# Hybrid encoder block on one core: where the casts of weights that are split ahead stand in ScalarE's order of issue

## The chip, the cores and the metric

The kernel runs on one core of a Trainium2 chip. A core has a matrix engine (TensorE, PE in the profile; PEld is its weight load), a vector engine (VectorE, DVE), a scalar engine (ScalarE, ACT), a general engine (GpSimd, POOL), a queue that only issues transfers (SyncE, SP), and sixteen DMA engines shared by all queues. The metric is device microseconds of the whole program, the median of several runs.

## The reference, cut to what matters

One layer of a streaming encoder works on 1024 tokens of width 1024, in float32. The part that this change touches is the input projection and what reads it:

```python
xn = rmsnorm(x, norm1_g[layer])
u = xn @ w_in[layer].astype(f32)
q_sb, k_sb, v_sb, f_raw, i_hg, q_hg, g_hg, gate_sb, gate_hg = jnp.split(u, list(c), axis=-1)
o_sb = stick_breaking_attention(split_heads(q_sb, SB_HEADS), ...)   # 8 heads of 64
o_hg = hgrn2_chunkwise(silu(q_hg), k_hg, i_hg, log_f)               # 4 heads of 128
merged = g_a * (o_sb @ w_o_sb) + g_b * (o_hg @ w_o_hg)
h = x + merged @ w_out
h = h + square(relu(rmsnorm(h) @ w_ff1)) @ w_ff2                    # width 4096
return rmsnorm(h, final_g)
```

Each w_in column block is used once, against all 1024 tokens.

## The kernel before, in words

**Split matmuls.** Every large product is made of three matmuls in a reduced format (`three`, L490). An operand becomes a high part h, cast by ScalarE (`hi_copy`, L141), and a low part l = x - h, subtracted by VectorE (`lo_sub`, L144). `hi_lo` (L150) does both. A tile of weights is 128 x 1024, so each split is one ScalarE cast and one VectorE subtraction.

**Units and buffers.** A `Unit` (L385) holds one block of weights. `load` (L401) brings the raw tile from memory into one of two buffers with the tag "raw"; `split` (L414) makes h and l in one of two buffers each, tags "whi" and "wlo". Wide units (`wide_unit`, L530: wv0, wv1, wi0, wi2) have two raw pieces and put their halves into the pool of 40 slots instead, so they hold no whi buffer. A `RawUnit` (L1110, wga0 to wga7, the gate weights) loads two raw tiles, splits one of them, subtracts twice in place and splits half of the result (`split_t`, tile t).

**Jobs.** `Stream` (L435) is the list of projection jobs. Its order is: wqk0 with wv0, wqk1 to wqk4, wv1, wqk5 to wqk7, then wf0, wq0, wi0, wg0, wf1, wq1, wg1, wga0, wf2, wq2, wi2, wg2, wga1, wga2, wf3, wq3, wg3, wga3 to wga7, wo00 to wo03. When a job starts (`_start`, L446), its units are already split, and `prefetch` (L454) splits the unit of the job behind it and loads the raw tile of the one after that. The gate jobs (`raw_job`, L1143) call `prefetch` inside their body, after their first twelve matmuls and the copy of the result (L1163) and its store from ScalarE's queue (L1164). In the first job it is called in the body too.

**Two lanes on TensorE.** The matmuls of the jobs are the lane "fill". The attention, and later the recurrence, is the lane "main": scores (bank z, sigmoids rm and bt on ScalarE), products along the row by a scan on VectorE, transposes (bank pw), their split into wTh and wTl, and the values (bank po); then the levels of the recurrence (sl, sd), with tails (pk, pkv, pho, pot). The program is written with one stretch of main, then some steps of fill, and so on. `open_block` (L103) keeps each lane in its own order and holds each stretch of fill behind the end of an earlier stretch of main (`AHEAD` = 2).

**What sets the order of issue.** Outside such edges a scheduler orders each engine's instructions when the program is built, by the order in which they are written and by its own estimate of when operands and buffers are there. On the chip each engine then runs its list in that order. `after(ins, earlier)` (L98) is an edge without a semaphore: the scheduler may not issue `ins` ahead of `earlier`, and nothing waits for it on the chip. `load` (L128) strings all of SP's loads into one order in this way. In the first microseconds ScalarE and VectorE follow a fixed turn (`in_turn`, L135).

So a cast in `prefetch` needs its raw tile landed and, in a whi buffer, the last matmul that read this buffer. With two buffers that is the last matmul of the job in front of the present one, where this job held a whi buffer. After a wide job, which holds none, the buffer is free a job earlier.

Of the kernel before, what the change touches and what calls it, by code (L numbers as in the profile page):

```python
# [39 lines left out]
def kernel(  # L40
# [19 lines left out]
    nc = tc.nc  # L60
# [14 lines left out]
    def slot(name, dt=F32):  # L75
        return spool.tile([P, 1024], dt, tag="s", name=name)
# [18 lines left out]
    lanes = {"main": Lane(), "fill": Lane()}  # L95
    cur = ["main"]

    def after(ins, earlier):  # L98
        if earlier is not None and earlier.ins is not ins.ins:
            tc.add_manual_dep(ins.ins, earlier.ins.name, NOSYNC, reason="issue order")  # L100
        return ins
# [30 lines left out]
    last_lo = [None]  # L132
    turns = {"on": False, "act": None, "dve": None}

    def in_turn(engine, ins):  # L135
        if turns["on"]:
            after(ins, turns[engine])
            turns[engine] = ins
        return ins

    def hi_copy(dst, src):  # L141
        in_turn("act", nc.scalar.copy(dst, src))  # L142

    def lo_sub(dst, src, hi):  # L144
        return in_turn(
            "dve",
            nc.vector.tensor_tensor(out=dst, in0=src, in1=hi.bitcast(F32), op=ALU.subtract),  # L147
        )

    def hi_lo(h, l, src):  # L150
        hi_copy(h, src)
        return lo_sub(l, src, h)

    def mul(out, a, b):
# [138 lines left out]
    class Quads:  # L293
# [42 lines left out]
        def split(self, i, kp, src, pr=0, n=4):  # L336
            if (i, kp) not in self.hl:
                self.hl[i, kp] = tuple(slot(f"sq{n_}{i}{kp}", F32R) for n_ in "hl")
            h, l = (self.part(t, pr, n) for t in self.hl[i, kp])
            self.last_lo = hi_lo(h, l, self.part(src, pr, n))  # L340
# [44 lines left out]
    class Unit:  # L385
# [25 lines left out]
                    load(dst[:, :, lo_c : lo_c + n], src)  # L411
                self.raw.append(r)

        def split(self, upto=None):  # L414
            self.load(upto)
            self.hl = self.hl or []
            for i, r in list(enumerate(self.raw))[len(self.hl) : upto]:
                if self.wide:
                    h = slot(f"{self.name}h{i}", F32R)
                    l = slot(f"{self.name}l{i}", F32R)  # L420
                else:
                    h = wpool.tile([P, 1024], F32R, tag="whi", name=f"{self.name}h{i}")
                    l = wpool.tile([P, 1024], F32R, tag="wlo", name=f"{self.name}l{i}")
                after(hi_lo(h, l, r), last_lo[0])
                self.hl.append((h, l))

    def cols_unit(name, parts):
# [7 lines left out]
    class Stream:  # L435
# [18 lines left out]
        def prefetch(self):  # L454
            nxt = []
            for us, _ in self.jobs[self.pos + 1 :]:
                nxt += [u for u in us if u.hl is None]
                if len(nxt) >= 2:
                    break
            if nxt:  # L460
                nxt[0].split()
                nxt[0].split_t()
            if len(nxt) > 1:
                nxt[1].load()
# [98 lines left out]
    def v_epilogue(quad):  # L563


        def ep(ps, tb):
            if tb % 2 == 0:
                vt[quad, tb // 2] = slot(f"V{quad}_{tb // 2}", F32R)
            V = vt[quad, tb // 2].rearrange("p (t h s d) -> p t h s d", t=2, h=4, s=2)
            src = ps.rearrange("p (h d) -> p h d", h=4)  # L570
            hi_lo(V[:, tb % 2, :, 0, :], V[:, tb % 2, :, 1, :], src)

        return ep
# [5 lines left out]
    def qk_epilogue(h):  # L579
        def ep(ps, half):  # L580
            if half == 0:
                qk[h] = tuple(slot(f"{n}{h}", F32R) for n in ("QH", "QL", "KS"))
            QH, QL, KS = qk[h]
            cs = slice(half * 512, (half + 1) * 512)
            hi_copy(KS[0:64, cs], ps[64:128])
            hi_copy(QH[0:64, cs], ps[0:64])
            lo_sub(KS[64:128, cs], ps[64:128], KS[0:64, cs])
            last_lo[0] = lo_sub(QL[0:64, cs], ps[0:64], QH[0:64, cs])
            for Q in (QH, QL):
                nc.gpsimd.dma_start(Q[64:128, cs].bitcast(F32), Q[0:64, cs].bitcast(F32))  # L590

        return ep
# [98 lines left out]
    def turn(h, qb, between):  # L691

        open_block("main")
        bt, rm = zs.pop((h, qb))
        qc, par = qb // 2, qb % 2
        nkb = 2 * qc + 2
        if (h, qc) not in wTt:
            wTt[h, qc] = [
                tuple(
                    slot_n(f"wT{n}{h}_{qc}_{k0}", 256 * min(nkb - k0, 4), F32R).rearrange(  # L700
                        "p (k q) -> p k q", q=256
                    )
                    for n in "hl"
                )
                for k0 in range(0, nkb, 4)
            ]
        tiles = wTt[h, qc]
        qs = slice(par * P, (par + 1) * P)
        if par == 0:
            for t in tiles[-1]:  # L710
                after(nc.gpsimd.memset(t[:, (nkb - 1) % 4, qs].bitcast(F32), 0.0), lastsel[0])
        order = list(enumerate(tiles))
        for i, (th, tl) in order[::-1] if qb == NT - 1 else order:
            n = min(qb + 1 - 4 * i, 4)
            if n <= 0:
                continue
            if qb == NT - 1 and i == 0:
                between()
                open_block("main")
            pw = bank(f"pw{h}_{qb}_{i}")  # L720
            for kb in range(n):
                s0 = (4 * i + kb) * P
                transpose(pw[:, kb * P : (kb + 1) * P], bt[:, s0 : s0 + P])
            turn_lo[0] = hi_lo(
                th[:, 0:n, qs], tl[:, 0:n, qs], pw[:, : n * P].rearrange("p (k q) -> p k q", q=P)
            )
        seen[h, qc] = seen.get((h, qc), 0) + 1
        return (h, qc) if seen[h, qc] == 2 else None
# [345 lines left out]
    def sub(out, a, b):  # L1074
        return nc.vector.tensor_tensor(out=out, in0=a, in1=b, op=ALU.subtract)
# [34 lines left out]
    class RawUnit(Unit):  # L1110
# [8 lines left out]
            ]  # L1119
            super().__init__(f"wga{cb}", dmas)  # L1120

        def split(self):
            if self.hl is not None:
                return
            self.load()
            ra, rb = self.raw
            h, l = (
                wpool.tile([P, 1024], F32R, tag=t, name=f"{self.name}{t}") for t in ("whi", "wlo")
            )
            hi_lo(h, l, ra)  # L1130
            sub(rb, ra, rb)
            sub(rb[:, 512:], rb[:, 512:], rb[:, 0:512])
            self.hl = [(h, l)]
# [62 lines left out]
    def sum_forms():  # L1196
# [11 lines left out]
        for kp in range(2):  # L1208
            s1[kp], s2[kp] = slot(f"gs1{kp}"), slot(f"gs2{kp}")
            ins = add(s1[kp], raw[1, 0, kp], raw[1, 1, kp])  # L1210
            if kp == 0:
                after(ins, hg_sum[0])
            yield
            sub(s2[kp], s1[kp], raw[0, 0, kp])
            yield
            split(6, kp, s2[kp])
            yield
        for kp in range(2):
            split(5, kp, s1[kp])
            yield  # L1220
        for kp in range(2):
            s3 = slot(f"gs3{kp}")
            sub(s3, raw[0, 0, kp], raw[1, 0, kp])
            yield
            split(7, kp, s3)
            yield
# [758 lines left out]
    for i, it in enumerate(items):  # L1985
# [16 lines left out]
        r = turn(*it, between)  # L2002
# [12 lines left out]
    for h in range(NHG + 1):  # L2015
        lev = hg_levels(h) if h < NHG else iter(())
        tail = hg_tail(h - 1) if h > 0 else iter(())
        upto = (j_hg[2], j_hg[3], j_raw[5], j_sb[1], j_sb[3])[h]
# [124 lines left out]
```

## Time and profile before

| what | before |
|---|---|
| median of three runs | 1470.97 us (1469.83 to 1471.96) |
| span of the profiled execution, its own time | 1469.2 us |
| mean granted TensorE clock | 0.993 |
| busy: PE, DVE, ACT, POOL | 98%, 75%, 46%, 9% |
| attention with projections, 12 to 320 us: PE, DVE, ACT busy | 301.93, 254.17, 193.08 us |
| recurrence with projections, 320 to 575 us: PE, DVE, ACT busy | 254.15, 194.84, 82.97 us |
| bytes moved by DMA | 227.30 MB, 155 GB/s on the mean |

The profile is of one execution. Its span runs from the first to the last instruction; the median of the runs is 1.8 us above it. A row of a timeline gives the start in us from the span's start, the duration in us, engine, line, operation, the tiles written and read (out<-in), the shape, and a count; in brackets stands how long the engine was idle before and what ended that. A row of a chain gives start, duration and what. A row of a tile gives the count, then the shortest, median and longest duration in ns, and the first and last start. A window's row gives the busy time of each engine, then the granted TensorE clock, the DMA share and GB/s. A matmul of 512 columns lasts 390 ns as listed, but starts follow each other at about 0.23 us, since matmuls are pipelined.

### The profile page before, as it was taken

The numbers are of one execution on the slowest core, as the hardware profiler recorded it, in microseconds if no ns is written. First come the engines' busy times: TensorE is split into PE (matmuls) and PEld (weight loads), VectorE is DVE, ScalarE is ACT, GpSimd is POOL, SyncE is SP. The second block draws the span as 40 slices with busy tenths as digits, with TensorE's granted clock in tenths as the row PEclk, the third lists the DMA queues.
The fourth block names the chain that finished last, engine by engine and source line by source line (L and its number), as shares of the span: only waits on it lengthen the run. The fifth ranks groups of instructions, "written<-read, shape, count | busy, mean of one in ns | idle before, by whom it ended". The sixth has DMA issues, their size and how long they took to land.

```text
span 1469.2 us, 20065 instructions
## 1 busy us (share of the span) xinstructions
PE 1441.4 (98%) x7490; PEld 1227.8 (84%) x7490; DVE 1105.7 (75%) x1591; ACT 671.9 (46%) x1180; POOL 132.0 (9%) x319
## 2 busy tenths in 40 slices
PE   8999998999999999999999899999999999999997
PEld 8889987988898888888888688888888888888886
DVE  6699797789657788877777888666766666768765
ACT  7566665552313234532344465444444533533433
POOL 3121111000000002100010300000000000000032
PEclk9999999999999999999999999999999999999999
DMA  7144255001313148665589223444444975676834
GB/s 206 35 119 101 46 106 110 27 15 44 93 30 100 51 129 234 227 208 179 170 270 302 101 79 123 158 158 158 157 157 158 345 272 201 231 276 246 281 104 179
DMA packets 157736, 227.30 MB, mean 155 GB/s; under 512 B 25308, under 2 KB 92936, under 8 KB 157640
## 3 DMA queue, kind: packets, MB, share of 16 engines
q1 hardware_dynamic: 142664, 184.07, 37.3%
q0 software_dynamic: 11376, 35.40, 9.3%
q10 hardware_dynamic: 3600, 6.56, 1.2%
q8 instruction: 59, 0.97, 0.3%
q14 instruction: 37, 0.30, 0.1%
HBM read 163.34 MB, written 62.65 MB: 154 GB/s over the span
## 4 chain that ended last, share of the span: by engine, by line
PE 89%; DVE 5%; DMA 2%; POOL 1%; issue 1%; ACT 1%; SPq 0%; POOLq 0%; ACTq 0%; DVEq 0%
PE pm L121 18%; PE pX L121 9%; PE pjqk L121 6%; PE pY L121 6%; PE pW L121 6%; PE pjv L121 3%; PE pys L121 3%; PE gY L121 3%; PE gX L121 3%; PE pyh L121 3%; PE pji L121 3%; PE pjg L121 3%; PE pjf L121 3%; PE po L121 3%; PE pjq L121 2%; PE z L121 2%
## 5 line engine op out<-in xcount | busy, mean ns | idle before, releaser
L142 ACT CAST whid<-w 128x1024 fp32r<-128x1024 f32 x31 | 32.6, 1052 | 154.1 <-PE pm L121 86.2
L679 DVE TENSOR_TENSOR_SCAN rm<-rm,bits 128x511 f32<-128x511 f32 (+7 forms) x72 | 87.3, 1219 | 15.2 <-ACT rm L657 13.5
L121 PE MATMUL pm<-wlod,sh 128*128 128x512 f32 x248 | 96.7, 390 | 0.7 <-DVE wlod L147 0.7
L121 PE MATMUL pm<-whid,sl 128*128 128x512 f32 x248 | 96.6, 390 | 0.0
L121 PE MATMUL pm<-whid,sh 128*128 128x512 f32 x248 | 96.6, 389 | 0.0
L147 DVE TENSOR_TENSOR wlod<-w,whid 128x1024 fp32r<-128x1024 f32 x31 | 37.9, 1223 | 57.2 <-ACT whid L142 57.2
L121 PE MATMUL pm<-th,sh 128*128 128x512 f32 x200 | 77.9, 390 | 0.0
L121 PE MATMUL pm<-th,sl 128*128 128x512 f32 x200 | 77.9, 389 | 0.0
L121 PE MATMUL pm<-tl,sh 128*128 128x512 f32 x200 | 77.9, 389 | 0.0
L147 DVE TENSOR_TENSOR sl<-sa,sh 128x1024 fp32r<-128x1024 f32 x56 | 68.3, 1219 | 0.8 <-ACT sh L142 0.8
L142 ACT CAST wTh<-pw 128x512 fp32r<-128x512 f32 (+3 forms) x96 | 44.4, 488 | 46.0 <-PE pw L124 40.4
L142 ACT CAST sh<-sa 128x1024 fp32r<-128x1024 f32 x56 | 57.2, 1046 | 10.9 <-DMA sa<-ad 10.9
L147 DVE TENSOR_TENSOR wTl<-pw,wTh 128x512 fp32r<-128x512 f32 (+3 forms) x96 | 50.8, 548 | 10.1 <-ACT wTh L142 5.6
L121 PEld LDWEIGHTS pm<-wlod,sh 128*128 128x128 f32 x248 | 46.6, 188 | 10.8 <-DVE wlod L147 1.1
L1809 POOL TENSOR_SCALAR fss<-fss 128x1 f32<-128x1 f32 x8 | 4.5, 561 | 563.0 <-ACT fsc L1804 562.5
L121 PEld LDWEIGHTS pm<-whid,sh 128*128 128x128 f32 x248 | 46.6, 188 | 9.6
L121 PEld LDWEIGHTS pm<-whid,sl 128*128 128x128 f32 x248 | 46.5, 188 | 9.6
L155 DVE TENSOR_TENSOR bt<-bt,rm 128x511 f32<-128x511 f32 (+7 forms) x72 | 48.9, 687 | 5.0 <-ACT wf0h L142 0.5
L657 ACT ACTIVATE rm<-z 128x511 f32<-128x511 f32 (+6 forms) x96 | 47.5, 502 | 5.8 <-DVE bt L155 2.6
L121 PE MATMUL pX<-sqh,t1h 128*128 128x512 f32 x128 | 49.9, 390 | 0.0
L121 PE MATMUL pX<-sql,t1h 128*128 128x512 f32 x128 | 49.9, 390 | 0.0
L121 PE MATMUL pX<-sqh,t1l 128*128 128x512 f32 x128 | 49.8, 389 | 0.0
(920 smaller groups left out, 4613.7 us busy)
## 6 DMA issues: line engine op xcount, KB each, us to landing
w<-in_w_ff_dram SPq DMA_DIRECT2D x72, 512.0 KB, 5.0
sa<-ad SPq DMA_DIRECT2D x56, 512.0 KB, 6.4
ad<-a SPq DMA_DIRECT2D x32, 256.0 KB, 4.2
ad<-s SPq DMA_DIRECT2D x16, 512.0 KB, 3.4
tw<-in_w_out_dram POOLq DMA_DIRECT2D x6, 1024.0 KB, 7.6
x<-in_x_dram SPq DMA_DIRECT2D x8, 512.0 KB, 9.4
xnl<-xnh POOLq DMA_DIRECT2D x8, 512.0 KB, 11.9
pr<-pd SPq DMA_DIRECT2D x8, 512.0 KB, 6.5
```

The source lines that it names most:

```text
L121: return pe(nc.tensor.matmul(*a, **k))
L142: in_turn("act", nc.scalar.copy(dst, src))
L147: nc.vector.tensor_tensor(out=dst, in0=src, in1=hi.bitcast(F32), op=ALU.subtract),
L155: return nc.vector.tensor_tensor(out=out, in0=a, in1=b, op=ALU.mult)
L657: nc.scalar.activation(rm[:, s0 + c0 - 1 : s0 + m - 1], z[:, c0:m], AF.Sigmoid, scale=-0.125)
L679: sc = nc.vector.tensor_tensor_scan(out=rr, data0=rr, data1=bits[:, 1024 - nk + a : 1024 - nk + b][:, ::-1], initial=rm[:, b : b + 1] if i ...
L1809: nc.gpsimd.tensor_scalar(out=ssq, in0=ssq, scalar1=1.0 / D, scalar2=EPS, op0=ALU.mult, op1=ALU.add)
```

## The change

`prefetch` hands `split` the last matmul that was issued in the fill lane, and the cast gets an edge without a semaphore behind it. At the start of a job that is the last matmul of the job in front; inside a gate job it is this job's own twelfth matmul. The VectorE subtraction has no new edge, and `split_t` has none. Splits outside `prefetch` are unchanged.

```diff
     def hi_copy(dst, src):
-        in_turn("act", nc.scalar.copy(dst, src))
+        return in_turn("act", nc.scalar.copy(dst, src))
...
-    def hi_lo(h, l, src):
-        hi_copy(h, src)
+    def hi_lo(h, l, src, hi_behind=None):
+        after(hi_copy(h, src), hi_behind)
         return lo_sub(l, src, h)
...
-        def split(self, upto=None):
+        def split(self, upto=None, hi_behind=None):
...
-                after(hi_lo(h, l, r), last_lo[0])
+                after(hi_lo(h, l, r, hi_behind), last_lo[0])
...
             if nxt:
-                nxt[0].split()
+                nxt[0].split(hi_behind=lanes["fill"].last)
                 nxt[0].split_t()
...
-        def split(self):
+        def split(self, upto=None, hi_behind=None):
             if self.hl is not None:
                 return
...
-            hi_lo(h, l, ra)
+            hi_lo(h, l, ra, hi_behind)
             sub(rb, ra, rb)
```

## The prediction

> **What bounds the kernel now.** I read the page's head first, for the span and for who is busy.
>
> ```profile
> span 1469.2 us, 20065 instructions
> PE 1441.4 (98%) x7490; PEld 1227.8 (84%) x7490; DVE 1105.7 (75%) x1591; ACT 671.9 (46%) x1180; POOL 132.0 (9%) x319
> ...
> PE 89%; DVE 5%; DMA 2%; POOL 1%; issue 1%; ACT 1%; SPq 0%; POOLq 0%; ACTq 0%; DVEq 0%
> ```
>
> TensorE is busy for 98% of the span and holds 89% of the chain that ended last. Moving work on ScalarE (ACT) can therefore pay only where TensorE stands still for it. Next I read ScalarE's waits, looking for casts of projection weights, and found one wait that reaches TensorE. The chain of waits between 240 and 266 us shows it whole:
>
> ```profile
> 243.98 9.09 DMA wg0r<-in_w_in_dram
> ...
> 253.09 1.05 ACT wg0h L142
> ...
> 255.32 0.69 DVE wTl L147
> ...
> 256.06 3.02 PE po L121 x12
> 259.07 1.49 PE z L121 x4
> 260.56 3.44 PE pjq L121 x12
> 264.01 0.44 PE pw L124 x4
> 264.44 0.95 PE po L121 x8
> ```
>
> The load of wg0's weights takes 9.09 us. ScalarE waits for it, casts wg0h, and only then produces what VectorE (DVE) and TensorE need for the attention. ScalarE's own timeline shows what stands behind that cast:
>
> ```profile
> 243.75 0.50 ACT L142 CAST wTh<-pw 128x384 fp32r<-128x384 f32 x1
> 253.09 1.04 ACT L142 CAST wg0h<-wg0r 128x1024 fp32r<-128x1024 f32 x1 [8.85 <-DMA wg0r<-in_w_in_dram]
> ...
> 258.92 0.60 ACT L799 ACTIVATE q<-pjq 128x512 f32<-128x512 f32 x1
> ```
>
> ScalarE sits idle for 8.85 us at the cast, though wg0 is used two jobs later: the present job is wq0 (bank pjq), then come wi0 and wg0. TensorE's timeline gives the price:
>
> ```profile
> 243.04 0.48 PE L121 MATMUL z<-KS,QH 128*128 128x512 f32 x1
> ...
> 244.06 0.39 PE L121 MATMUL pjq<-xnh,wq0h 128*128 128x512 f32 x1
> ...
> 246.79 0.71 PE L124 MATMUL pw<-ident,bt 128*128 128x128 f32 x5
> ...
> 247.58 0.40 PE L121 MATMUL pjq<-xnh,wq0h 128*128 128x512 f32 x1
> ...
> 250.31 0.60 PE L124 MATMUL pw<-ident,bt 128*128 128x128 f32 x4
> 256.06 0.58 PE L121 MATMUL po<-wTh,V 128*128 128x256 f32 x1 [5.14 <-DVE wTl L147]
> ...
> 263.85 0.60 PE L124 MATMUL pw<-ident,bt 128*128 128x128 f32 x4
> ```
>
> After the transposes at 250.31 TensorE idles 5.14 us, because the transposed weights of 246.79 were never evacuated. It then runs slowly, as the windows with the granted clock show:
>
> ```profile
> 256.00:262.00 6.00, 5.95 (x20) 5.43 (x21) 5.86 (x10) 3.42 (x8) 0.38 (x3) 0.51 0.29 87
> 262.00:268.00 6.00, 6.00 (x43) 5.52 (x42) 5.17 (x6) 4.19 (x11) 0.45 (x5) 1.00 0.10 26
> ```
>
> The granted clock is 0.51 in the first six microseconds after the stall and 1.00 in the next six.
>
> **The change, part by part.** Nothing is computed that was not computed before. The number of casts, subtractions, loads and matmuls stays; what moves is the place of a cast in ScalarE's order, and with it its VectorE subtraction and the loads that wait for the raw buffer. The edge carries no semaphore, so it adds no wait on the chip by itself.
>
> *wg0h, the term that pays.* The prefetch that casts wg0h is written at the start of job wi0, so the last matmul in front of it is the last of wq0. Is the cast ahead of that matmul today? Yes: in ScalarE's timeline it stands ahead even of q<-pjq at 258.92, which reads the first half of wq0, so it was issued while wq0 was still running. After the change it stands behind the last matmul of the second half. Then ScalarE goes from 244.25 straight to the transposed weights of 246.79 and TensorE need not stop. The stretch from 250.31 to 263.85, two starts of transposes, is 13.54 us. At full clock the same work costs: four transposes, 264.01 to 264.44, 0.43; twelve po matmuls at 0.95/8 each, 1.42; four z matmuls, two of 512 and two of 384 columns, 7/8 of the 1.02 from 243.04 to 244.06, 0.89; twelve pjq matmuls, 247.58 to 250.31, 2.73. Together 5.47 us, so the loss is 13.54 - 5.47 = **8.1 us**: 5.14 idle, and about 2.9 of slow clock (0.49 of 6 us).
>
> The Trainium skill, "TensorE: Matmul & The Clock Gate", Part 1 (What's actually happening), says that TensorE falls to half rate after an idle window of about 3.4 us and needs about 3.4 us of work to come back. By that the slow part would cost 1.7 us and the gain would be 6.8, an estimate from the page. The trace agrees on the mechanism, but its slow stretch is nearer 6 us, so I keep the measured 8.1.
>
> What is late next? The wg0 load is unchanged (buffer freed by wi0's first subtraction) and lands at 253.07 (243.98 + 9.09). In the new timeline the last wq0 matmul ends about 264.0 - 8.1 = 255.9, so the cast finds its data there with some 2.8 us to spare. If ScalarE reaches it earlier it waits again, but then behind the evacuations that TensorE needs.
>
> *The other casts.* For jobs whose forerunner held one of the two whi buffers the cast already waits for exactly that last matmul, so nothing changes. It moves where the forerunner is wide (its halves lie in slots) or where a gate job prefetches inside its own body. For the wide ones I looked at when the weights are used:
>
> ```profile
> L121 PE MATMUL pjv<-wv1h,xnl x64: 278/283/287, 126.1 to 163.0; 128*128 128x256 f32 x64
> ...
> L121 PE MATMUL pjqk<-xnh,wqk6h x16: 387/390/401, 182.5 to 198.4; 128*128 128x512 f32 x16
> ...
> L121 PE MATMUL pji<-wi0h,xnl x64: 279/283/286, 266.1 to 302.3; 128*128 128x256 f32 x64
> ...
> L121 PE MATMUL pjf<-xnh,wf1h x16: 389/390/478, 321.1 to 336.1; 128*128 128x512 f32 x16
> ...
> L147 DVE TENSOR_TENSOR wf1l<-wf1r,wf1h x1: 1227/1227/1227, 264.9 to 264.9; 128x1024 fp32r<-128x1024 f32 x1
> ...
> L121 PE MATMUL pji<-wi2h,xnl x64: 280/283/287, 406.6 to 435.0; 128*128 128x256 f32 x64
> ...
> L121 PE MATMUL pga<-xnh,wga1whi x8: 388/390/394, 449.1 to 458.3; 128*128 128x512 f32 x8
> ```
>
> From the last wide matmul to the first use there remain 182.5 - 163.0 = 19.5 us for wqk6, 18.8 for wf1 and 14.1 for wga1. A cast (1.05) and its subtraction (1.23) need 2.3. (wqk2 behind the first job is of the same sort; I quote no row for it.) These cost nothing; the cover is the whole job between, and without it each would cost at most its 2.3 us.
>
> The gate jobs are tighter. At wga0 the cast of wf2h moves from the job's start behind its twelfth matmul:
>
> ```profile
> 371.07 0.59 ACT L1163 COPY p<-pga 128x512 f32<-128x512 f32 x1 [1.01 <-PE pga L121]
> ...
> 376.29 1.05 ACT L142 CAST wq2h<-wq2r 128x1024 fp32r<-128x1024 f32 x1 [4.62 <-PE pga L121]
> ...
> 373.86 0.69 DVE L1072 TENSOR_TENSOR p<-p,pgq 128x512 f32<-128x512 f32 x1 [2.38 <-PE pgq L121]
> ...
> 376.31 0.39 PE L121 MATMUL pjf<-xnh,wf2h 128*128 128x512 f32 x1
> ```
>
> The copy at 371.07 was released by that matmul. Behind it: copy to 371.66, the issue of the copy's store on ScalarE's queue (not in these rows; bounded by 0 and by one more copy, 0.59; I take 0.35), cast to 373.1, subtraction to 374.3. ScalarE idles 4.62 us and VectorE 2.38 us just there. TensorE wants wf2h at 376.31: **2 us to spare, cost 0**. The same shape recurs for wga2, wf3, wga4, wga5 and wga6.
>
> *The loads.* A later cast frees its raw buffer later, and every load on SP's queue behind it follows (the loads keep one order). The place where that could bite is wga5:
>
> ```profile
> 516.99 1.22 DVE L147 TENSOR_TENSOR wga4wlo<-wga4r,wga4whi 128x1024 fp32r<-128x1024 f32 x1
> ...
> 518.28 0.59 ACT L1163 COPY p<-pga 128x512 f32<-128x512 f32 x1 [0.64 <-PE pga L121]
> ...
> 518.24 1.57 SPq L129 DMA_DIRECT2D wga5r<-in_w_in_dram  x2
> ...
> 525.10 1.23 DVE L1075 TENSOR_TENSOR wga5r<-wga5r,wga5r 128x1024 f32<-128x1024 f32 x1 [1.96 <-DMA wga5r<-in_w_in_dram]
> ```
>
> Today the first load goes out when wga4wlo ends, 518.2. With the cast behind the copy of 518.28 the subtraction ends at 518.87 + 1.05 + 1.23 = 521.2, so the loads go out 2.9 us later, and VectorE, which already waits 1.96 us for them, would wait up to 4.9. Queued behind that instruction is the work of the recurrence levels that TensorE reads. The cost lies between 0 and 2.9 us; the nearest row is VectorE's existing 1.96 us wait, which stops nobody in TensorE's timeline, so I take 0 and keep 2.9 for the range.
>
> The Trainium skill, "DMA: Bandwidth & Descriptors", Rules for kernel authors, advises issuing a DMA early and waiting for it late. It speaks on both sides here: the change waits later at wg0, but it also issues loads later. No run here has measured the second part.
>
> *Sum.* 1469.2 - 8.1 = 1461.1 us of span. The median is 1470.97, which is 1.8 above this span; that is what lies around it and the run's own spread, and I carry it over: 1470.97 - 8.1 = 1462.9.
>
> **The rivals.** *Part is given back.* Late loads or a rearranged order of VectorE take 2 to 5 us: 1465 to 1468. For it: VectorE's wait at 525.10 grows. Against it: the idle times in the rows above.
>
> *Another wait takes the place.* ScalarE's order is laid out at compile time. If some cast lands again ahead of evacuations while its load is under way, one stall of the size of wg0's (8.1) comes back: 1471. The edge without effect gives the same number; against that stands q<-pjq, behind wg0h today.
>
> *Slower.* At a gate job the cast could land not directly behind the twelfth matmul but behind the cast and sigmoid that wait for the job's end, as wq2h does at 376.29. Then TensorE, done at about 376.3, waits for wq2h 1.05, the sigmoid (bounded by the 0.59 copy from below, taken as 0.7), wf2h 1.05 and the subtraction 1.23: 4.0 us. It decides from the point where the cast is over 2.0 us later than worked out above. Six such places are 24 us: 1470.97 - 8.1 + 24 = 1487; three are enough to be slower, at 1475. Against it: ScalarE is idle for 4.62 us exactly where the cast would go.
>
> **How the numbers follow.** The forecast, 8.1 gained and nothing else touched, has 0.57 and its own range is 1461 to 1465. Part given back has 0.13, another wait or no effect 0.14, slower 0.16. A measurement of this kernel can tell about 0.2%, 2.9 us, from no change. Faster: 0.57 + 0.13 = 0.70; same 0.14; slower 0.16. The range goes from 1461 (the forecast less the 1.1 us of spread among the three runs, and a little) to 1472, which takes in the second rival and leaves out the third.
>
> **What would show it.** Right: ScalarE no longer waits for wg0r; the granted clock between 250 and 262 us is 1.00; the first wi0 matmul of the row above comes 8 us earlier than 266.1; wf1h is cast after wi0 ends, near 294 in the new timeline; wf2's first matmul follows wga0's last without idle time. Wrong: a new idle time of TensorE over 1 us between 30 and 580 us, above all in front of pjf or pga, or released by a load of wga5; or a different order of the blocks on TensorE itself, which I have taken to stay as it is.

## The result and the profile after

| what | before | after |
|---|---|---|
| median, measured together (four runs each) | 1470.72 us (1469.83 to 1471.96) | 1461.88 us (1460.90 to 1462.87) |
| ratio | | 0.994 (95%: 0.9927 to 0.9952) |
| span of the profiled execution | 1469.2 us | 1460.8 us |
| mean granted TensorE clock | 0.993 | 0.997 |

The changed kernel is faster by 8.8 us, 0.6%. A second measurement of it gave 1462.05 against 1470.69 us, ratio 0.9943 (0.9931 to 0.9956). In the first 600 us, where the casts moved, TensorE works through its blocks in the same order as before. The head of the page:

```profile
span 1460.8 us, 20051 instructions
PE 1437.6 (98%) x7490; PEld 1224.0 (84%) x7490; DVE 1105.9 (76%) x1591; ACT 671.5 (46%) x1180; POOL 132.9 (9%) x319
...
PE 92%; DVE 4%; POOL 1%; issue 1%; DMA 1%; ACT 1%; SPq 0%; POOLq 0%; DVEq 0%; ACTq 0%
```

No engine has less to do: VectorE and ScalarE are busy as long as before. TensorE is busy 3.8 us less for the same matmuls, in good part because fewer of them run at a slow clock, as will be seen. What went is waiting. Of the chain that ended last, DMA had 2% and has 1%, VectorE had 5% and has 4%. TensorE's waits, grouped by what they waited for, show which one (total us, times, longest us). First before, then after:

```profile
PE po L121 <- DVE wTl L147: 6.5, 4, 5.1
```

```profile
PE po L121 <- DVE wTl L147: 1.2, 3, 0.6
```

One wait of 5.1 us is gone. ScalarE's timeline of the changed kernel at this place:

```profile
246.47 0.59 ACT L142 CAST wTh<-pw 128x512 fp32r<-128x512 f32 x1 [3.19 <-PE pw L124]
...
254.14 1.05 ACT L142 CAST wg0h<-wg0r 128x1024 fp32r<-128x1024 f32 x1
255.30 0.60 ACT L799 ACTIVATE q<-pjq 128x512 f32<-128x512 f32 x1
```

The first transposed weights are cast at 246.47, as soon as TensorE has made them. The cast of wg0h stands at 254.14 with no wait in brackets: its load, which went out at 243.02 and took 9.1 us as before, has landed. It is now followed directly by the evacuation of the second half of wq0, and the earlier ones stand ahead of it. TensorE's timeline, whose rows answer to those of the prediction:

```profile
249.35 0.60 PE L124 MATMUL pw<-ident,bt 128*128 128x128 f32 x4
249.71 0.36 PE L121 MATMUL po<-wTh,V 128*128 128x256 f32 x1
...
255.10 0.60 PE L124 MATMUL pw<-ident,bt 128*128 128x128 f32 x4
```

The po matmul starts 0.36 us behind the transposes' start, where it was 5.75 (250.31 to 256.06). From po to the next transposes it takes 5.39 us, where it took 7.79 (256.06 to 263.85). So the stretch went from 13.54 to 5.75 us: **5.39 us by the wait and 2.40 by the clock, 7.79 together**. The windows confirm the clock, the third column from the right:

```profile
250.00:256.00 6.00, 6.00 (x36) 5.13 (x35) 5.82 (x9) 5.03 (x9) 0.38 (x3) 1.00 0.51 137
256.00:262.00 6.00, 6.00 (x51) 5.91 (x50) 5.45 (x9) 3.23 (x8) 0.45 (x5) 1.00 0.30 89
```

To see whether the rest of the kernel moved, I use two distant points. Rows of the first and the last start of a group, before:

```profile
L121 PE MATMUL pjqk<-xnh,wqk1h x16: 388/390/396, 54.5 to 66.7; 128*128 128x512 f32 x16
...
L121 PE MATMUL pji<-wi0h,xnh x64: 277/283/286, 265.9 to 302.1; 128*128 128x256 f32 x64
```

And after, with the cast of wf1h:

```profile
L121 PE MATMUL pjqk<-xnh,wqk1h x16: 387/389/395, 54.3 to 66.5; 128*128 128x512 f32 x16
...
L121 PE MATMUL pji<-wi0h,xnh x64: 277/283/285, 257.2 to 293.3; 128*128 128x256 f32 x64
...
L142 ACT CAST wf1h<-wf1r x1: 1055/1055/1055, 294.9 to 294.9; 128x1024 fp32r<-128x1024 f32 x1
```

From the first wqk1 matmul to the first wi0 matmul it took 211.4 us and takes 202.9: 8.5 less. The stall's stretch gives 7.8 of it; 0.7 comes from elsewhere. Behind this point little changes: the span is 8.4 us shorter.

### The profile page after: what moved, and what is told of

Read it like the earlier page. It is cut to its first block, busy times and chain, and to the rows that moved or that the text cites. A ratio compares the mean times of both kernels' runs of the same rounds, so it can differ in the third digit from the quotient of the medians.

```text
span 1460.8 us, 20051 instructions
## 1 busy us (share of the span) xinstructions
PE 1437.6 (98%) x7490; PEld 1224.0 (84%) x7490; DVE 1105.9 (76%) x1591; ACT 671.5 (46%) x1180; POOL 132.9 (9%) x319
## 4 chain that ended last, share of the span: by engine, by line
PE 92%; DVE 4%; POOL 1%; issue 1%; DMA 1%; ACT 1%; SPq 0%; POOLq 0%; DVEq 0%; ACTq 0%
PE pm L121 18%; PE pX L121 9%; PE pY L121 6%; PE pW L121 6%; PE pjqk L121 6%; PE pjv L121 3%; PE pga L121 3%; PE pjq L121 3%; PE pys L121 3%; PE pyh L121 3%; PE gY L121 3%; PE gX L121 3%; PE pji L121 3%; PE pjf L121 3%; PE pjg L121 3%; PE po L121 3%
## 5 line engine op out<-in xcount | busy, mean ns | idle before, releaser
L142 ACT CAST wTh<-pw 128x128 fp32r<-128x128 f32 (+3 forms) x96 | 44.4, 487 | 50.1 <-PE pw L124 45.2
```

The source lines that it names most:

```text
L142: return in_turn("act", nc.scalar.copy(dst, src))
```

## The experiments

The theory was that of the prediction: the cast of wg0h, waiting for its load, keeps ScalarE from the evacuations that TensorE needs. The rivals: that the other moved casts bring a good part of the gain; that it is VectorE's subtraction of wg0, not ScalarE's cast, that stands in the way; that the place of the cast matters and not its wait. Two sizes were open as well: what part of the 8 us is the slow clock, and what a gate job's cast costs when it comes too late. All kernels were timed in five rounds against the kernel before; the table gives its median beside theirs.

| kernel | median | before, measured with it | ratio (95%) |
|---|---|---|---|
| edge for wg0 alone | 1463.16 | 1470.48 | 0.995 (0.9938 to 0.9963) |
| edge for all but wg0 | 1469.80 | 1470.48 | 0.9996 (0.9987 to 1.0005) |
| edge on the subtraction only | 1468.57 | 1470.48 | 0.999 (0.9981 to 0.9999) |
| before, wg0's raw tile in slots | 1464.04 | 1470.50 | 0.9955 (0.9942 to 0.9967) |
| before, wg0 loaded twice | 1470.04 | 1470.50 | 0.9999 (0.999 to 1.0008) |
| before, 22 matmuls in a spare bank | 1477.31 | 1470.48 | 1.0045 (1.0033 to 1.0058) |
| the same, bank taken earlier | 1478.02 | 1470.50 | 1.0054 (1.004 to 1.0068) |
| before, 22 matmuls into pjq's bank | 1470.12 | 1470.69 | 0.9997 (0.9988 to 1.0006) |
| after, gate jobs' prefetch later | 1464.54 | 1470.50 | 0.9961 (0.9948 to 0.9973) |
| after, gate jobs' prefetch last | 1472.58 | 1470.69 | 1.0016 (1.0007 to 1.0025) |
| after, no edge for wqk2 | 1461.55 | 1469.80 | 0.9946 (0.9932 to 0.9959) |
| after, once more | 1462.05 | 1470.69 | 0.9943 (0.9931 to 0.9956) |

**One edge alone, and all the others alone.** The first kernel keeps the edge for wg0 only:

```diff
-                nxt[0].split(hi_behind=lanes["fill"].last)
+                nxt[0].split(hi_behind=lanes["fill"].last if nxt[0].name == "wg0" else None)
```

> The changed kernel with the edge on the cast of wg0h alone; all other casts stand as before. Theory (one cast blocks ScalarE behind a load of 9.09 us, and TensorE pays 5.14 us idle and 2.9 us of slow clock for it): the whole gain, 8.1 to 8.8 us below the kernel before, so about 1462, and no wait of ScalarE for wg0r. Rival (the gain is spread over the dozen casts that moved): a part of it only, 1464 to 1469.

The second keeps all the others:

```diff
-                nxt[0].split(hi_behind=lanes["fill"].last)
+                nxt[0].split(hi_behind=None if nxt[0].name == "wg0" else lanes["fill"].last)
```

> The changed kernel with the edge on every cast that is split ahead except wg0h. Theory: the stall stays, within 1.5 us of the kernel before (1470.7), with TensorE idle about 5 us before po and a granted clock near 0.5 after it. Rival (spread): 1463 to 1468.

The first gained 7.3 us, the second 0.7. Together they make the 8.0 that is nearly the whole effect. In the first, the stretch from transposes to transposes is 5.76 us (251.47 to 257.23), as in the changed kernel. In the second ScalarE waits and TensorE stands still as before. Rows of ScalarE's and TensorE's timelines:

```profile
252.12 1.04 ACT L142 CAST wg0h<-wg0r 128x1024 fp32r<-128x1024 f32 x1 [8.69 <-DMA wg0r<-in_w_in_dram]
```

```profile
249.51 0.60 PE L124 MATMUL pw<-ident,bt 128*128 128x128 f32 x4
255.08 0.58 PE L121 MATMUL po<-wTh,V 128*128 128x256 f32 x1 [4.96 <-DVE wTl L147]
...
261.71 0.60 PE L124 MATMUL pw<-ident,bt 128*128 128x128 f32 x4
```

But here the work from po to the next transposes took 6.63 us (255.08 to 261.71) and not 7.79. The windows with the granted clock tell why. Before, and then this kernel:

```profile
253.50:257.00 3.50, 0.94 (x4) 0.95 (x5) 2.83 (x3) 3.09 (x8) 0.00 (x0) 0.73 0.08 23
257.00:260.50 3.50, 3.50 (x15) 3.30 (x14) 3.40 (x8) 1.94 (x4) 0.38 (x3) 0.50 0.44 133
260.50:264.00 3.50, 3.50 (x15) 2.79 (x14) 3.42 (x4) 1.16 (x3) 0.00 (x0) 0.80 0.03 7
```

```profile
253.50:257.00 3.50, 1.92 (x9) 1.92 (x10) 3.50 (x5) 2.14 (x8) 0.00 (x0) 0.71 0.36 106
257.00:260.50 3.50, 3.50 (x16) 3.08 (x16) 3.40 (x7) 2.29 (x5) 0.38 (x3) 0.80 0.15 44
260.50:264.00 3.50, 3.50 (x26) 3.20 (x26) 3.28 (x4) 1.96 (x5) 0.45 (x5) 1.00 0.02 5
```

Before, the clock is short by 0.27, 0.50 and 0.20 of 3.5 us, 3.4 us in all, which at half speed is a slow stretch of 6.8 us. In the second kernel it is short by 0.29 and 0.20, 1.7 us, a slow stretch of 3.4. The same stall is followed in one execution by twice as long a slow stretch as in the other. Its price is 7.79 - 5.39 = 2.4 us in the one and 6.63 - 5.39 = 1.2 in the other, with the changed kernel's 5.39 for the full clock.

The other casts, then, gained 0.7 us (between 1.9 gained and 0.7 lost). The timing alone doesn't tell that from nothing. The profiles do: the way from the first wqk1 matmul to the first wi0 matmul is 203.7 us with the edge on wg0 alone (55.6 to 259.3) and 202.9 with all of them.

**The subtraction, not the cast.** The edge is moved from ScalarE's cast to VectorE's subtraction:

```diff
-        after(hi_copy(h, src), hi_behind)
-        return lo_sub(l, src, h)
+        hi_copy(h, src)
+        return after(lo_sub(l, src, h), hi_behind)
```

> The edge put on VectorE's subtraction in place of ScalarE's cast, so that wg0h still stands early on ScalarE and only wg0l is held back on VectorE. Theory (ScalarE's queue is what blocks): no gain, within 1.5 us of 1470.7, ScalarE still idle about 9 us for wg0r. Rival (VectorE's wait of 6.21 us for wg0h is what blocks TensorE, since wTl stands behind wg0l): most of the gain, 1462 to 1465.

It gained 1.9 us of 8.8, a little more than the 1.5 that the theory allowed and far less than its rival asked for. One row each of ScalarE, VectorE and TensorE:

```profile
251.39 1.04 ACT L142 CAST wg0h<-wg0r 128x1024 fp32r<-128x1024 f32 x1 [8.66 <-DMA wg0r<-in_w_in_dram]
```

```profile
252.95 0.69 DVE L147 TENSOR_TENSOR wTl<-pw,wTh 128x512 fp32r<-128x512 f32 x1 [6.49 <-ACT wTh L142]
```

```profile
253.70 0.38 PE L121 MATMUL po<-wTh,V 128*128 128x256 f32 x1 [4.29 <-DVE wTl L147]
```

ScalarE waits 8.66 us for the load, VectorE 6.49 for ScalarE, TensorE 4.29 for VectorE: the stall is handed down the line. Taking wg0's subtraction out of VectorE's way shortens the last of them from 5.14 to 4.29. The rest comes from ScalarE's queue, and this rival falls. The edge stands on all moved subtractions here, so the 1.9 us are not wg0's alone.

**The place kept, the wait taken away.** In the kernel before, wg0's raw tile is put into the slots pool, so that its load needn't wait for the other raw buffers and can have landed when ScalarE comes to the cast:

```diff
+            if u.name == "wg0":
+                u.roomy = (0,)
```

> The kernel before, without any new edge; the raw weights of wg0 get a place of their own in the pool of slots, so that their load need not wait for wi0's subtraction and goes out 20 us earlier; the cast stays early in ScalarE's order. Theory (the price is ScalarE's wait for this one load, not the early place of the cast): the same gain as with the edge, 1462 to 1464, cast of wg0h with no wait. Rival (an early cast hurts in itself, as work ahead of the evacuations): at most half of the gain, 1466 to 1470.

It gained 6.5 us without any edge. The load's issue on SP and the cast on ScalarE:

```profile
240.12 0.37 SPq L129 DMA_DIRECT2D wg0r<-in_w_in_dram  x1
```

```profile
243.99 1.05 ACT L142 CAST wg0h<-wg0r 128x1024 fp32r<-128x1024 f32 x1
```

The cast stands as early as before, ahead of the evacuations, but no wait stands in its row, and the stretch from transposes to transposes is 5.75 us (250.15 to 255.90). So a cast in this place costs nothing; a cast that waits does. The way from wqk1 to wi0 is 203.7 us, as with the edge on wg0 alone. The load went out 3.9 us earlier than before (243.98) and not 20 us earlier as I had thought: the loads on SP still keep one order. That alone would not have been enough. At 9.09 us the load would have landed at 249.2, but here it took 3.8 us and landed just ahead of the cast. In the kernel before, a transfer of 1 MB (tw<-tw, from GpSimd's queue) went out at 240.74, 3.2 us ahead of this load; here it goes out at 247.87, when the load has landed. That this transfer is what makes the load take 9 us fits, but no run isolates it.

**The wait made longer.** In the kernel before, wg0 is loaded twice into the same tile, so that the data come later:

```diff
                     load(dst[:, :, lo_c : lo_c + n], src)
+                    if self.name == "wg0":
+                        load(dst[:, :, lo_c : lo_c + n], src)
```

> The kernel before with wg0's raw weights loaded twice, one load behind the other into the same tile, so that they are there some 4 to 9 us later. No edge; but the order that is laid out at compile time then has the cast of wg0h behind the evacuation of the transposes of 246.79 and five more instructions of ScalarE. Theory (what counts is what stands behind the waiting cast, not how long the load takes): no stall before the first po any more, a wait of ScalarE of 10 us or more all the same, a smaller stall later at the transposes of 250.31; 1463 to 1468, less than before although the load takes longer. Rival (the time of the load is what is paid): 4 to 9 us more than before, 1475 to 1480.

Time: 1470.04, no change. Neither theory had said so, though the first had the new place of the cast right. ScalarE's and TensorE's timelines:

```profile
247.20 0.59 ACT L142 CAST wTh<-pw 128x512 fp32r<-128x512 f32 x1 [3.19 <-PE pw L124]
...
256.60 1.04 ACT L142 CAST wg0h<-wg0r 128x1024 fp32r<-128x1024 f32 x1 [7.33 <-DMA wg0r<-in_w_in_dram]
```

```profile
250.08 0.60 PE L124 MATMUL pw<-ident,bt 128*128 128x128 f32 x4
...
260.76 1.11 PE L124 MATMUL pw<-ident,bt 128*128 128x128 f32 x4 [4.78 <-DVE bt L155]
```

The scheduler, which goes by its own estimate of when the data are there, put the cast further back, behind the evacuation of 247.20 and five more instructions. There it still waited 7.33 us. The first po matmul no longer stalled, but the stall of TensorE came one step later, at the transposes of 260.76, and cost 4.78 us of idle time, about as much as before and not less. So this run didn't double the suspected cost; it moved it. The order on ScalarE follows the estimate, which the second load changed, and in both places the waiting cast stalled TensorE through the work behind it.

**How much is the slow clock?** To keep TensorE's clock up through the stall of the kernel before, 22 matmuls without use were put ahead of the po matmul, first into a bank of their own:

```diff
+        if (h, qc) == (5, 2):
+            spare = bank("spare")
+            for _ in range(22):
+                matmul(spare, v_stat(h, 0), vt[h // 4, 0][:, 0:512], start=True, stop=True)
```

> The kernel before with 22 extra matmuls of 512 columns on TensorE just in front of the po matmuls that stall; they write a spare bank that nobody reads, and the order on all other engines is that of before. At 0.228 us each they take 5.0 us, so they fill the 5.14 us of idle time with work and the stall itself stays as long. Theory (2.9 of the 8.1 us are slow clock that follows from the idle time): granted clock 1.00 from 250 to 268 us and 2.5 to 3.3 us less than before, about 1467.8. Rival (the slow clock costs nothing here, the idle time is all): same as before, 1470.7, or slower by what the filling overshoots.

It came out 6.8 us slower than before. The reason is in TensorE's timeline:

```profile
257.41 6.72 PE L121 MATMUL spare<-V 128*128 128x512 f32 x22 [5.40 <-DVE wTl L147]
```

The fillers themselves waited 5.40 us for the same VectorE instruction, and ran when the stall was over. I read this as follows: the bank that they were given was one that the stalled evacuations had not yet emptied. So I had it taken earlier, with one matmul at the start of the turn before, so that it was held when the stall began:

```diff
+        if (h, qb) == (5, 4):
+            spare.append(bank("spare"))
+            matmul(spare[0], v_stat(5, 0), vt[1, 0][:, 0:512], start=True, stop=True)
...
+        if (h, qc) == (5, 2):
+            for _ in range(22):
+                matmul(spare[0], v_stat(5, 0), vt[1, 0][:, 0:512], start=True, stop=True)
```

> The kernel before with the same 22 extra matmuls of 512 columns in front of the stalled po, this time into a spare bank that is taken one stretch earlier (by one more matmul), so that the filling has nothing to wait for; nobody reads it. The filling takes 22 x 0.228 = 5.0 us of the 5.14 us of idle time. Theory (slow clock follows the idle time, 3.4 or 6.8 us at half rate by the clock records so far): granted clock 1.00 from 250 to 268 us, TensorE idle under 1 us before po, 1.5 to 3.3 us less than the kernel before, 1467 to 1469. Rival (the slow clock costs nothing): 1470.5 to 1471.

Now the transposes ahead of the fillers stood still, 5.42 us for wTl until 256.39, and the kernel took 7.5 us more than before. Both kernels missed their purpose and say nothing on the clock. They fit banks that the stall holds too: with one bank taken, the transposes lack it. No run shows the state of the banks. The third try takes no bank: the 22 matmuls go into the bank that the q projection is just filling.

```diff
+            running[0] = (ps, wh[:, c : c + P], xh)
...
+        if (h, qc) == (5, 2):
+            for _ in range(22):
+                matmul(*running[0], start=False, stop=False)
```

> The kernel before with 22 extra matmuls of 512 columns in front of the stalled po; this time they add into the bank of the running wq0 product, which is held anyway, so they need no free bank (the q projection of the first head is computed wrongly by that). The two earlier fillings waited themselves for a bank that VectorE had not read out. Theory (idle time brings 3.4 or 6.8 us at half clock behind it): TensorE idle under 1 us before po, granted clock 1.00 from 250 to 268 us, 1.5 to 3.3 us less than before, 1467 to 1469. Rival (the slow clock costs nothing): 1470.5 to 1471.

TensorE's timeline and its windows:

```profile
251.69 5.24 PE L121 MATMUL pjq<-xnh,wq0h 128*128 128x512 f32 x22
...
257.15 0.39 PE L121 MATMUL po<-wTh,V 128*128 128x256 f32 x1 [0.22 <-DVE wTl L147]
...
262.55 0.60 PE L124 MATMUL pw<-ident,bt 128*128 128x128 f32 x4
```

```profile
251.00:257.00 6.00, 5.93 (x29) 4.59 (x27) 1.73 (x2) 2.82 (x7) 0.00 (x0) 1.00 0.66 175
257.00:263.00 6.00, 5.85 (x33) 5.02 (x34) 5.86 (x11) 3.42 (x9) 0.38 (x3) 1.00 0.30 87
```

The fillers end just as wTl comes, the granted clock stays at 1.00, and from po to the next transposes it takes 5.40 us (257.15 to 262.55), the 5.39 of the changed kernel. So with the stall in place and the clock kept up, the slow part of 2.4 or 1.2 us is gone. The median fell by only 0.6 us (between 1.8 less and 0.9 more), which missed what was expected. In the profiles the way from wqk1 to wi0 fell from 211.4 to 209.1 us, but wi0's own matmuls then took 36.8 us from first to last where they took 36.2, so 0.6 us were given back. Whether the stretch is mostly the short or the long one stays open. Of six profiles with a stall of 4.3 to 5.4 us at or near this place, five show the short one and only the kernel before the long one. But the granted clock of the whole program was 0.9940 on the mean over 21 executions of the kernel before and 0.9966 over 11 of this one; 0.26% of 1470 us is 3.8 us of full clock, as much as the long stretch takes (3.4).

**The gate jobs' casts later.** In the changed kernel the prefetch of a gate job was put behind the job's second part, and in a further kernel at its very end, written behind the sigmoid that waits for its last matmul:

```diff
-            st.prefetch()
...
             add(p14, p1, p4)
+            st.prefetch()
```

> The changed kernel with the prefetch of the gate jobs moved behind their next twelve matmuls, so that the casts there stand at least 2.9 us later, and some loads too. The prediction gave those casts 2 us to spare behind the twelfth matmul. Theory of the prediction: TensorE now waits about 1 us at some of the eight gate jobs, 1463 to 1470 in all. Rival (the casts run ahead of that matmul, since the edge holds no wait, and have more to spare): within 1.5 us of the changed kernel, about 1462.

```diff
-            st.prefetch()
...
                 a_sb.put(cb - 4, osb[cb - 4])
+            st.prefetch()
```

> The changed kernel with the prefetch of the gate jobs moved to the end of their bodies, so that the cast of the next weights stands behind the cast or sigmoid that wait for the job's last matmul: the place of the prediction's third rival. Its price was 4.0 us at each place. Theory (that price is right): eight places, 8 x 2.3 (cast and subtraction alone) to 8 x 4.0 us more than the changed kernel, 1480 to 1494, TensorE waiting 2.3 to 4.0 us at the start of each job behind a gate job. Rival (the recurrence's matmuls between the jobs cover it): under 1470.

The first took 1464.54 us, 2.5 above the changed kernel's 1462.05, which was measured at another time. The intervals of the two ratios overlap, so that the timing alone doesn't settle it; TensorE's timeline shows 1.5 us of new idle time, 0.96 for wga7whi at 556.42 and 0.53 for wga7wlo at 557.68, in front of the last gate job. Behind the other gate jobs no new wait shows.

The second took 1472.58, 10.5 above the changed kernel (1462.05, measured with it), between its theory and its rival, and the whole gain is lost. TensorE's waits:

```profile
PE pga L121 <- DVE wga7wlo L147: 2.5, 1, 2.5
...
PE pga L121 <- ACT wga6whi L142: 1.6, 1, 1.6
PE pga L121 <- DVE wga6wlo L147: 1.3, 1, 1.3
...
PE pys L121 <- DVE wo00l L147: 0.9, 1, 0.9
PE pga L121 <- DVE wga2wlo L147: 0.8, 1, 0.8
...
PE pga L121 <- DVE wga4wlo L147: 0.8, 1, 0.8
```

These are 7.9 us of idle time in five places, none above 2.9. But the casts do not stand where the theory wanted them. ScalarE's rows at wga0:

```profile
363.59 1.05 ACT L142 CAST wf2h<-wf2r 128x1024 fp32r<-128x1024 f32 x1 [0.41 <-ACT p L1163]
368.09 0.69 ACT L1173 ACTIVATE g<-pga,prm 128x512 f32<-128x512 f32 x1 [3.44 <-PE pga L121]
```

The cast of wf2h, though written behind the sigmoid (L1173), was put ahead of it. So were six more of the eight. Only wga6whi stands behind its sigmoid (546.66 behind 546.08), and there TensorE's waits come to 2.9 us (1.6 and 1.3), not 4.0. The price of the prediction's rival is thus measured in one place and not in eight. These kernels move the prefetch's loads along with its casts, so they price the place of the whole prefetch.

**wqk2.** Only the edge of wqk2's cast is taken out of the changed kernel:

```diff
-                nxt[0].split(hi_behind=lanes["fill"].last)
+                nxt[0].split(hi_behind=None if nxt[0].name == "wqk2" else lanes["fill"].last)
```

> The changed kernel without the edge on the cast of wqk2h, which in the changed kernel moves from 41 to 57 us into the first scans of the attention and stands in front of a stall of 0.56 us at 70.5 us (0.59 us in all against the kernel before, between TensorE's first wqk1 and first wi0 matmul). Theory (that move is the only one of the dozen that costs): the way from the first wqk1 to the first wi0 matmul 202.3 us in the profile in place of 202.87, the time 1461.3 to 1462.5, too near the changed kernel (1462.05) to tell from it by the median. Rival (the stall comes from another of the moved casts): the way stays at 202.87.

The way from the first wqk1 matmul to the first wi0 matmul is 202.3 us (55.7 to 258.0) instead of 202.9, so this one moved cast costs some 0.6 us. The profiles of other kernels agree: the first matmuls of wqk2 and wqk3 lie 20.7 to 20.8 us apart in the three with this edge and 20.1 to 20.2 in five without it. In the changed kernel TensorE waits 0.32 us at its place, in a row that the kernel before doesn't have:

```profile
70.50 0.38 PE L121 MATMUL po<-wTl,V 128*128 128x256 f32 x1 [0.32 <-DVE wTl L147]
```

The median, 1461.55, can't be told from that of the changed kernel.

**The changed kernel again.**

> The changed kernel itself, on the chip of the other runs of this call. Theory (wg0h alone carries the gain): 1461.5 to 1463.5, 7 to 9 us below the kernel before, not to be told from the kernel with the edge on wg0h alone (1463.16). Rival (the other casts bring over 1.5 us more): below 1461.5.

1462.05 us, with the same stretch of 5.74 us between transposes and the same way of 202.9 us.

## Why the prediction was right, step by step

**The wait that pays** was named rightly: one cast, one load, one place. The forecast was 1462.9 and 1461.88 was measured. The edge on wg0 alone gave 7.3 of the 8.8 us and the others alone 0.7. That it is the wait and not the place, and ScalarE and not VectorE, was assumed there and is now shown, by the kernel in which the load is there in time (6.5 gained without an edge) and by the edge on the subtraction (1.9). The load was to be there 2.8 us ahead of the cast; it was 2.0 us (landed at 252.1, cast at 254.14).

**Its size** was right in the sum, 8.1 against 7.8 measured in the profiled pair, and its two terms were each a little off. The idle term of 5.14 was 5.39 as lateness of po. The term that was mis-sized is "about 2.9 of slow clock". It was what was left of the stretch beside the idle time and the work at full clock, and the full-clock price of the stretch was set at 5.47 where the changed kernel needs 5.75 (from the first po matmul to the first z, 249.71 to 251.51, it takes 1.80 and not 1.42). It measures 2.4 in that execution and 1.2 in one of the kernel with all other edges. By the Trainium skill, "TensorE: Matmul & The Clock Gate", Part 1 (What's actually happening), the rate is set by an activity window of 3.413 us that runs freely, and the number of slow matmuls varies from run to run by its phase at the kernel's start. The traces fit this: the slow stretches were 3.4 and 6.8 us, one window and two. The 1.7 us estimated from the page reckons with one window; I had set it aside for 2.9, and it lies between the two prices measured.

**The other casts** were costed at nothing. They are not quite: 0.7 us gained in the profiles before wi0, in which wqk2, which I mentioned with no row and cost at nothing, has lost some 0.6. The starts of the jobs show where the gain is: from wv1's first matmul to wqk5's it takes 36.9 us in place of 38.0, the same 36.9 to 37.0 in four profiles with these edges and 38.0 to 38.1 in four without. A wait of TensorE of 0.45 us at 135.93 (po for wTl) is gone there. Two casts moved out of this stretch or within it, wqk5h (from 117.5 to 123.5) and wqk6h (from 123.8 to 162.0); no run separates them. wqk5h was not on my list at all. I had said that a cast moves only behind a wide job or inside a gate job. It moves also when it is split ahead in a wide job itself, which is the case of wg0h, and so of wqk5h in wv1 and of wg2h in wi2, whose cast moved 10.2 us towards its use. It is by chance that this gain makes up for the 0.3 us by which the stall was overestimated.

**The gate jobs** were to have 2 us to spare. At wga0 they have about 4, since the edge asks for less than I thought. In the changed kernel, ScalarE's rows, VectorE's and TensorE's at wga0:

```profile
361.27 1.05 ACT L142 CAST wf2h<-wf2r 128x1024 fp32r<-128x1024 f32 x1
362.37 0.59 ACT L1163 COPY p<-pga 128x512 f32<-128x512 f32 x1
```

```profile
362.35 1.23 DVE L147 TENSOR_TENSOR wf2l<-wf2r,wf2h 128x1024 fp32r<-128x1024 f32 x1 [0.24 <-ACT wf2h L142]
```

```profile
367.61 0.39 PE L121 MATMUL pjf<-xnh,wf2h 128*128 128x512 f32 x1
```

I had put the cast behind the copy that waits for the twelfth matmul. It stands ahead of that copy: the edge only says that the cast is issued after this matmul has been issued, and on the chip it waits for nothing. The subtraction ends at 363.6, and wf2's first matmul, at 367.61 with no bracket, follows the job's last without idle time, 4 us later. The cost of nothing was right, its working was not. The kernel with the gate jobs' prefetch later has wf2h where I had put it, directly behind the copy, at 364.81. There VectorE comes to the subtraction only at 367.20, behind its work on the job's second part, and ends it at 368.42; wf2's first matmul at 369.05 has no idle time in front. So in that place too the cost is nothing, but with some 0.6 us to spare and not 2.

**The loads of wga5** were to go out 2.9 us later against the work around them. They don't. The cast of wga4whi on ScalarE and the issue of these loads on SP:

```profile
507.86 1.05 ACT L142 CAST wga4whi<-wga4r 128x1024 fp32r<-128x1024 f32 x1
...
510.87 0.61 ACT L1163 COPY p<-pga 128x512 f32<-128x512 f32 x1
```

```profile
509.40 1.50 SPq L129 DMA_DIRECT2D wga5r<-in_w_in_dram  x2
```

The loads go out 8.8 us earlier than the 518.24 of before, as much earlier as TensorE's matmuls of wga5 (528.3 instead of 537.0). The reason is that of wga0: the cast stands ahead of the copy and not behind it. So the cost of 0 was right for a reason that I hadn't seen. One load did go out much later, wg1r at 298.07 and not at 266.15, behind the moved cast of wf1h, and no cast waits for it. What later loads of the gate jobs would cost stays unmeasured on their own.

**What would show it** came as listed: no ScalarE wait for wg0r, a granted clock of 1.00 between 250 and 262, wi0's first matmul 8.7 us earlier, wf1h cast at 294.9, TensorE's order unchanged.

**The rivals.** "Part is given back" and "another wait takes the place" did not happen. The slower one did not happen either: in the changed kernel the casts of the gate jobs stand ahead of the copy. Its price stays largely untested. With the prefetch at the end of all eight gate jobs the kernel comes out at 1472.58, 10.5 us above the changed one, but only wga6whi then stood where this rival puts its six casts, and cost 2.9 us and not 4.0. wf2, on whose rows the 4.0 was built, shows no wait of TensorE, because its cast still ran ahead of the sigmoid.

## What to carry to other kernels

An engine that runs its list in order pays for a wait with everything that stands behind the waiting instruction. So, before moving a prefetch's conversion, look in the timeline for the bracket that names a DMA, and follow what is queued behind it down to the engine that sets the end: here 8.85 us of ScalarE's idle time became 5.14 of TensorE's, and both a later cast and a load that was there in time removed it. Of the other casts that moved, none waited more than 0.70 us for its load (wga7whi and wo00h), and together they were worth 0.7 us. And an edge in the order of issue only forbids a place; where the cast then stands has to be read from the new timeline. A stall's price is its idle time and a slow stretch behind it, which is best taken from the same work at full clock and not from the mean clock of a window.

## What the hardware showed beside

- After a stall of about 5 us, TensorE ran at half clock for 6.8 us in an execution of the kernel before and for 3.4 in one of the kernel with all edges but wg0's, at a price of 2.4 and 1.2 us. One profile doesn't tell this price to better than 1 us.
- In one of three tries, matmuls without use kept the granted clock at 1.00 through a stall of 5.4 us: when they were written into a bank that was already being filled. In a bank of their own they waited for the stall to end (5.40 us) or made the transposes wait (5.42), and cost 6.8 and 7.5 us.
